# Eleven joint additions in place of fourteen, and shorter lookups, in the expert routing of a hybrid encoder layer

## The chip, the cores and the metric

The kernel runs on one core of one Trainium2 chip. The time is the device time of one execution in microseconds (us); lower is better. A core has a matrix engine (TensorE, PE in the profile; PEld is its weight load), a vector engine (VectorE, DVE), an activation engine (ScalarE, ACT), a general engine (GpSimd, POOL), a queue engine (SyncE, SP) and 16 DMA engines. Each engine works through its own list of instructions in order and waits on semaphores.

## The reference, cut to what matters

One layer over 1024 tokens of width 1024: layer norm, attention beside a long convolution, an output projection, layer norm, then a feed-forward part that picks experts, and a last layer norm. The change lies in the picking. For each token and each of 8 heads there are two lists of 128 scores; the 16 best of each list are summed in all pairs, and the 16 best pairs name the experts:

```python
sv, si = lax.top_k(s, PEER_TOPK)                                   # 16 of 128, two lists a head
cand = sv[:, :, 0, :, None] + sv[:, :, 1, None, :]
cidx = si[:, :, 0, :, None] * PEER_NKEYS + si[:, :, 1, None, :]    # PEER_NKEYS = 128
best, pos = lax.top_k(cand.reshape(C, PEER_HEADS, 256), PEER_TOPK)
eidx = jnp.take_along_axis(cidx.reshape(C, PEER_HEADS, 256), pos, axis=-1)
g = jax.nn.softmax(best, axis=-1)
u = u_tab[eidx]; vv = v_tab[eidx]                                  # 16384 experts of width 1024
a = gelu(einsum('chkd,cd->chk', u, xc))
out = einsum('chk,chkd->cd', g * a, vv)
```

All of it is fp32.

## The kernel before

The 1024 tokens are 8 tiles of 128. Three tiles (the gathered ones) fetch their 128 expert rows of each token from the tables by indirect DMA on POOL (`gather`): a row set arrives in one of six buffers `grow`, and VectorE makes a dot product of it (line 1262) or adds it to `gacc` (line 1270). The other five tiles (the dense ones) go through all 16384 experts: `u_part` multiplies a slice of 128 experts with the tokens on TensorE, after the slice has been split in two parts `uh` (ScalarE) and `ul` (VectorE, the helper at lines 290 to 292); the result, weighted by a table that `build_g` makes from the picked experts, is multiplied with the V table in the last part of the kernel (`weigh`, `v_group`).

The picking is `route(tt, rp, done)`, called once for each of the 8 tiles, always through tiles with one buffer each. Its work is on VectorE almost alone:

- lines 1022 to 1027: the 16 best values `r_sv` and their numbers `r_si` in each of 16 lists of 128 scores, by two rounds of MAX8, FIND_INDEX8 and one MATCH_REPLACE8;
- lines 1031 and 1036: the numbers cast to fp32 (`r_sf`), those of the first list times 128;
- lines 1037 to 1045: of the 256 pairs only the 50 can be among the best 16 whose ranks a, b (from 0) have (a+1)(b+1) at most 16. They are laid out as seven rectangular blocks of ranks, and one addition a block writes the sums to `r_cand`, another the expert numbers to `r_cidx`;
- lines 1048 to 1053: the 16 best of the 50 and their positions `r_pos`;
- lines 1059 to 1067: lookup of the expert number at each position: a comparison of all positions 0 to n-1 with the position wanted, a product with the numbers, and a sum (`r_oh`, `r_ef`). The best four can only lie in the first 16 candidates, the next four in the first 32;
- from line 1069: the softmax, and for a dense tile the numbers in the form that `build_g` needs.

`route` is a generator: it hands back the control after each piece, and `weights` interleaves the pieces with those of `build_g`, paced against the first 72 of the 128 calls of `u_part`. The first routing runs beside the last scores; the other seven run beside those 72 slices, first those of the dense tiles, then those of two gathered tiles. That order in the program is only a start: `TileContext(nc, schedule_with_timeline_sim=True)` lets a planner order each engine's list by its own estimate of when things are ready, and place the waits. After the 72 slices, the kernel goes on with the remaining 56, the weighting (`gt` loads the table) and the V table.

Of the kernel before, what the change touches and what calls it, by code (L numbers as in the profile page):

```python
# [10 lines left out]
F32 = mybir.dt.float32  # L11
# [5 lines left out]
ALU = mybir.AluOpType  # L17
AX = mybir.AxisListType
# [3 lines left out]
P = 128  # L22
# [273 lines left out]
def layer(ctx: ExitStack, tc: tile.TileContext, a: dict, out: bass.AP):  # L296
    nc = tc.nc
# [268 lines left out]
    for j in (*range(4, 12), *range(4)):  # L566
        u = pjp.tile([P, T], F32, name="u", bufs=1)
        project(4 + j, u)
        y = z_sb[:, j] if j < 4 else pjp.tile([P, T], F32, name="gt_y", bufs=1)
        nc.scalar.activation(y, u, AF.Identity, bias=sb[:, j:j + 1], scale=sw[:, j, 1:2])  # L570
        nc.vector.scalar_tensor_tensor(y[:, 1:T], u[:, 0:T - 1], sw[:, j, 0:1], y[:, 1:T],
                                       op0=ALU.mult, op1=ALU.add)
        nc.vector.scalar_tensor_tensor(y[:, 0:T - 1], u[:, 1:T], sw[:, j, 2:3], y[:, 0:T - 1],
                                       op0=ALU.mult, op1=ALU.add)
# [158 lines left out]
    with tc.tile_pool(name="ltp", bufs=2, side="right") as ltp:  # L733
# [70 lines left out]
        for c in range(2):  # L804
# [6 lines left out]
            for tt in range(0, NT, 2):  # L811
                ps = bank()
                for e in range(2):
                    s = slice((tt + e) * P, (tt + e + 1) * P)
# [110 lines left out]
    iota = keep.tile([P, P], F32, name="iota")  # L925
# [78 lines left out]
    NEG = -3.0e38  # L1004
    NCAND = 50

    blocks = [(0, 4, 0, 4), (0, 2, 4, 4), (4, 4, 0, 2), (0, 1, 8, 8), (8, 8, 0, 1), (2, 1, 4, 1), (4, 1, 2, 1)]
    finds = [(0, 8, 0, 4, 16), (0, 8, 4, 8, 32), (0, 4, 8, 16, NCAND), (4, 8, 8, 16, NCAND)]  # L1010

    routed = []
    CHUNK = 55.0 / 12
# [1 line left out]
    def route(tt, rp, done):  # L1015


        s = rp.tile([P, 16, P], F32, name="r_s")
        nc.sync.dma_start(s, s_d[tt].rearrange("p h (q n) -> p (h q) n", q=2))
        sv = rp.tile([P, 16, 16], F32, name="r_sv")  # L1020
        si = rp.tile([P, 16, 16], U32, name="r_si")
        for g in range(16):
            nc.vector.max(sv[:, g, 0:8], s[:, g])
            nc.vector.max_index(si[:, g, 0:8], sv[:, g, 0:8], s[:, g])
            nc.vector.match_replace(s[:, g], sv[:, g, 0:8], s[:, g], NEG)
            nc.vector.max(sv[:, g, 8:16], s[:, g])
            nc.vector.max_index(si[:, g, 8:16], sv[:, g, 8:16], s[:, g])
            if g % 3 == 2:
                yield CHUNK
        sf = rp.tile([P, 16, 16], F32, name="r_sf")  # L1030
        nc.vector.tensor_copy(sf, si)
        cand = rp.tile([P, 8, NCAND], F32, name="r_cand")
        cidx = rp.tile([P, 8, NCAND], F32, name="r_cidx")
        sv4 = sv.rearrange("p (h q) k -> p h q k", q=2)
        sf4 = sf.rearrange("p (h q) k -> p h q k", q=2)
        nc.vector.tensor_scalar(sf4[:, :, 0], sf4[:, :, 0], 128.0, None, op0=ALU.mult)
        for eng, dst, src in ((nc.vector, cand, sv4), (nc.vector, cidx, sf4)):
            off = 0
            for a0, na, b0, nb in blocks:
                o = dst[:, :, off:off + na * nb].rearrange("p h (x y) -> p h x y", y=nb)  # L1040
                x = src[:, :, 0, a0:a0 + na].unsqueeze(3).to_broadcast([P, 8, na, nb])
                y = src[:, :, 1, b0:b0 + nb].unsqueeze(2).to_broadcast([P, 8, na, nb])
                eng.tensor_add(o, x, y)
                off += na * nb
            assert off == NCAND
        best = rp.tile([P, 8, 16], F32, name="r_best")
        pos = rp.tile([P, 8, 16], U32, name="r_pos")
        for h in range(8):
            nc.vector.max(best[:, h, 0:8], cand[:, h])
            nc.vector.max_index(pos[:, h, 0:8], best[:, h, 0:8], cand[:, h])  # L1050
            nc.vector.match_replace(cand[:, h], best[:, h, 0:8], cand[:, h], NEG)
            nc.vector.max(best[:, h, 8:16], cand[:, h])
            nc.vector.max_index(pos[:, h, 8:16], best[:, h, 8:16], cand[:, h])
            if h % 4 == 3:
                yield CHUNK
        pf = rp.tile([P, 8, 16], F32, name="r_pf")
        nc.vector.tensor_copy(pf, pos)
        ef = rp.tile([P, 8, 16], F32, name="r_ef")
        for h0, h1, k0, k1, n in finds:
            nh, nk = h1 - h0, k1 - k0  # L1060
            oh = rp.tile([P, 32 * NCAND], F32, name="r_oh")[:, 0:nh * nk * n]
            oh = oh.rearrange("p (h k n) -> p h k n", h=nh, k=nk)
            nc.vector.tensor_tensor(
                oh, iota[:, 0:n].unsqueeze(1).unsqueeze(1).to_broadcast([P, nh, nk, n]),
                pf[:, h0:h1, k0:k1].unsqueeze(3).to_broadcast([P, nh, nk, n]), op=ALU.is_equal)
            nc.vector.tensor_mul(oh, oh, cidx[:, h0:h1, 0:n].unsqueeze(2).to_broadcast([P, nh, nk, n]))
            nc.vector.reduce_sum(ef[:, h0:h1, k0:k1], oh, axis=AX.X)
            yield CHUNK
        w = rp.tile([P, 8, 16], F32, name="r_w")
        nc.vector.tensor_sub(w, best, best[:, :, 0:1].to_broadcast([P, 8, 16]))  # L1070
        nc.scalar.activation(w, w, AF.Exp)
        den = rp.tile([P, 8], F32, name="r_den")
        nc.vector.reduce_sum(den, w, axis=AX.X)
        nc.vector.reciprocal(den, den)
        den_b = den.unsqueeze(2).to_broadcast([P, 8, 16])
        ef2 = ef.rearrange("p h k -> p (h k)")
        if tt < NG:
            nc.vector.tensor_copy(eid[tt], ef2)
            nc.vector.tensor_mul(gat[tt].rearrange("p (h k) -> p h k", k=16), w, den_b)
            routed.append(tt)  # L1080
            return
        nc.vector.tensor_mul(w, w, den_b)
        ei = rp.tile([P, P], I32, name="r_ei")
        nc.vector.tensor_copy(ei, ef2)
        ij = rp.tile([P, 2, P], I32, name="r_ij")
        nc.vector.tensor_scalar(ij[:, 0], ei, 7, None, op0=ALU.arith_shift_right)
        nc.vector.tensor_scalar(ij[:, 1], ei, 127, None, op0=ALU.bitwise_and)
        ijf = rp.tile([P, P], F32, name="r_ijf")
        nc.vector.tensor_copy(ijf, ij[:, 0])
        jj = rp.tile([P, P], I32, name="r_jj")  # L1090
        nc.vector.tensor_tensor(jj, ij[:, 1], ij[:, 1], op=ALU.mult)
        jp = rp.tile([P, 2, P], I32, name="r_jp")
        nc.vector.tensor_scalar(jp[:, 1], jj, 127, None, op0=ALU.bitwise_and)
        nc.vector.tensor_scalar(jp[:, 0], jj, 127 << 7, None, op0=ALU.bitwise_and)
        jx = rp.tile([P, 3, P], BF16, name="r_jx")
        nc.vector.tensor_copy(jx[:, 0], ij[:, 1])
        nc.vector.tensor_copy(jx[:, 1:3], jp)
        nc.sync.dma_start(jx_d[tt].rearrange("r t s -> t r s"), jx)
        jl = jls[tt % 2]
        for r in range(3):  # L1100
            nc.sync.dma_start(jl[32 * r:32 * r + 32], jx_d[tt, r].rearrange("(q t) s -> t q s", t=32))
        ps = psO.tile([P, 2, P], F32, name="ps_o0")
        nc.tensor.transpose(ps[:, 0], ijf, ident)
        nc.tensor.transpose(ps[:, 1], w.rearrange("p h k -> p (h k)"), ident)
        ig = rp.tile([P, 2, P], F32, name="ig", bufs=2)
        nc.scalar.copy(ig, ps)
        done.append((ig, jl))
        yield CHUNK
# [196 lines left out]
    with tc.tile_pool(name="rp", bufs=1, side="left") as rp, \  # L1305
# [9 lines left out]
        for jl in jls:  # L1315
            nc.gpsimd.memset(jl[96:98], 1.0)
        r0 = route(0, rp, [])
        for _ in scores(hd, NG, DENSE):
            with tc.issue_after(normed[-1].ins):
# [7 lines left out]
        def weights():  # L1327


            done = []  # L1330
            yield from route(NG, rp, done)
            for t in range(DENSE):
                beside = route(NG + t + 1, rp, done) if t + 1 < DENSE else route(1, rp, done)
                for n, c in enumerate(build_g(done[t], t, gp)):
                    yield c
                    if n % 5 in (0, 2, 4):
                        yield next(beside, 0.0)
                yield from beside
            for g in range(2, NG):
                yield from route(g, rp, done)  # L1340
# [214 lines left out]
```

## Time and profile before

| | us |
|---|---|
| median of 3 runs | 3274.26 |
| lowest and highest | 3264.43, 3280.19 |
| profiled execution, its own time | 3255.75 |
| span of the profile, first to last instruction | 3254.0 |

The profile is of one execution. Busy times are sums over instructions of an engine; TensorE's matmuls overlap one another, and their ends are modelled. The granted TensorE clock over the span is 0.962 of full speed. 44798 instructions were recorded, 5514 of them on VectorE.

### The profile page before, as it was taken

Reading aid. Unit: us, or ns where it says so; the run is one execution under the profiler, and the core shown is the slowest. Engines: PE = TensorE matmul, PEld = TensorE weight load, DVE = VectorE, ACT = ScalarE, POOL = GpSimd, SP = SyncE. Lnnn points to the kernel's source line nnn. Section 1 sums busy time; section 2 is a strip of 40 time slices with the busy share of each in tenths; the row PEclk is TensorE's granted clock in tenths of the full one; section 3 lists DMA queues with packets and bytes.
Section 4 is the critical chain, followed back from the end, with each engine's and each line's share of the span. In section 5 each row is a group of like instructions: output and inputs, shape, how many; then the busy total and the mean of one; then the engine's idle time right before and its main releaser. Section 6 shows DMA issues by size and latency. Waiting matters only on the chain.

```text
span 3254.0 us, 44798 instructions
## 1 busy us (share of the span) xinstructions
PE 2988.5 (92%) x15582; PEld 2552.1 (78%) x15582; DVE 2735.7 (84%) x5514; ACT 1256.2 (39%) x2454; POOL 1036.4 (32%) x797
## 2 busy tenths in 40 slices
PE   6999898889999779999999789998999999799997
PEld 5677676556689778999898778886888888588886
DVE  7556799888757799999999768888889879888888
ACT  4544344455523216766574122222222222122222
POOL 0000000000000351332435735555555445455551
PEclk9999889989999989999999899999999999999998
DMA  5244743322444777887888999999999999989995
GB/s 173 97 149 133 249 123 104 102 56 73 138 152 149 278 252 241 302 303 277 310 284 319 364 338 336 325 358 341 329 358 323 353 315 333 337 302 353 342 332 188
DMA packets 355064, 828.87 MB, mean 255 GB/s; under 512 B 34345, under 2 KB 144851, under 8 KB 351253
## 3 DMA queue, kind: packets, MB, share of 16 engines
q0 software_dynamic: 110592, 402.70, 34.5%
q1 hardware_dynamic: 230709, 356.71, 33.9%
q10 hardware_dynamic: 13536, 66.59, 5.2%
q8 instruction: 123, 2.02, 0.2%
q14 instruction: 104, 0.85, 0.1%
HBM read 715.52 MB, written 110.33 MB: 254 GB/s over the span
## 4 chain that ended last, share of the span: by engine, by line
PE 31%; DVE 22%; DMA 7%; issue 6%; POOL 3%; ACT 1%; SPq 0%; DVEq 0%; POOLq 0%; ACTq 0%
PE ps_x L285 5%; PE ps_x L287 5%; PE ps_x L286 5%; DVE grow L1262 4%; DVE gacc L1270 4%; DMA vr<-in_peer_v 3%; PE ps_h L285 3%; PE ps_h L287 3%; PE ps_h L286 3%; POOL grow L1249 3%; DVE p L1160 2%; PE ps_o L285 2%; PE ps_o L286 2%; PE ps_o L287 2%; DVE ul L292 2%
## 5 line engine op out<-in xcount | busy, mean ns | idle before, releaser
L1249 POOL DMA_INDIRECT grow<-in_peer_u,eid x384 | 518.0, 1349 | 582.3 <-DVE grow L1262 206.9
L1249 POOL DMA_INDIRECT grow<-in_peer_v,eid x384 | 504.8, 1315 | 606.1 <-DVE gacc L1270 267.3
L1270 DVE SCALAR_TENSOR_TENSOR gacc<-grow,dot,gacc 128x1024 f32<-128x1024 f32 x381 | 487.3, 1279 | 13.2 <-DMA grow<-in_peer_v,eid 9.6
L1262 DVE SCALAR_TENSOR_TENSOR grow<-grow,gh 128x1024 f32<-128x1024 f32 x384 | 460.1, 1218 | 19.8 <-DMA grow<-in_peer_u,eid 19.5
L287 PE MATMUL ps_x<-hd,ul 128*128 128x320 f32 x1152 | 368.3, 328 | 50.1 <-DVE ul L292 49.7
L285 PE MATMUL ps_x<-hd,uh 128*128 128x320 f32 x1152 | 373.6, 325 | 28.4 <-ACT uh L291 26.2
L286 PE MATMUL ps_x<-hd,uh 128*128 128x320 f32 x1152 | 370.3, 322 | 0.0
L286 PE MATMUL ps_x<-vl,wh 128*128 128x512 f32 x864 | 341.1, 395 | 1.7 <-DVE vl L292 1.6
L287 PE MATMUL ps_x<-vh,wl 128*128 128x512 f32 x864 | 336.8, 393 | 0.0
L285 PE MATMUL ps_x<-vh,wh 128*128 128x512 f32 x864 | 302.3, 396 | 28.4 <-ACT vh L291 23.2
L291 ACT CAST vh<-vr 128x512 fp32r<-128x512 f32 x256 | 156.3, 619 | 388.4 <-DMA vr<-in_peer_v 280.6
L285 PE MATMUL ps_h<-hd,uh 128*128 128x320 f32 x896 | 278.8, 311 | 9.0 <-ACT A L1221 5.6
L286 PE MATMUL ps_h<-hd,uh 128*128 128x320 f32 x896 | 278.3, 311 | 0.0
L287 PE MATMUL ps_h<-hd,ul 128*128 128x320 f32 x896 | 275.8, 311 | 2.5 <-DVE ul L292 2.5
L287 PEld LDWEIGHTS ps_x<-hd,ul 128*128 128x128 f32 x1152 | 222.7, 195 | 65.0 <-DVE ul L292 59.0
L285 PEld LDWEIGHTS ps_x<-hd,uh 128*128 128x128 f32 x1152 | 225.9, 196 | 35.4 <-ACT uh L291 31.8
L292 DVE TENSOR_TENSOR vl<-vr,vh 128x512 fp32r<-128x512 f32 x256 | 174.5, 687 | 75.7 <-ACT vh L291 74.4
L286 PEld LDWEIGHTS ps_x<-hd,uh 128*128 128x128 f32 x1152 | 225.8, 196 | 0.8
L291 ACT CAST uh<-ur 128x1024 fp32r<-128x1024 f32 x128 | 134.7, 1052 | 223.7 <-DMA ur<-in_peer_uT 103.1
L285 PEld LDWEIGHTS ps_x<-vh,wh 128*128 128x128 f32 x864 | 162.7, 190 | 63.5 <-ACT vh L291 24.7
L292 DVE TENSOR_TENSOR ul<-ur,uh 128x1024 fp32r<-128x1024 f32 x128 | 155.5, 1215 | 63.8 <-ACT uh L291 62.4
L286 PEld LDWEIGHTS ps_x<-vl,wh 128*128 128x128 f32 x864 | 164.4, 190 | 37.1 <-DVE vl L292 4.4
(366 smaller groups left out, 6876.3 us busy)
## 6 DMA issues: line engine op xcount, KB each, us to landing
ur<-in_peer_uT SPq DMA_DIRECT2D x128, 512.0 KB
vr<-in_peer_v SPq DMA_DIRECT2D x256, 256.0 KB
g_d<-gst ACTq DMA_DIRECT2D x20, 2048.0 KB
gt<-g_d SPq DMA_DIRECT2D x32, 1280.0 KB
a_d<-A ACTq DMA_DIRECT2D x72, 320.0 KB
A<-a_d SPq DMA_DIRECT2D x72, 320.0 KB
fw<-in_dft_fw SPq DMA_DIRECT2D x64, 256.0 KB
wr<-in_w_in SPq DMA_DIRECT2D x16, 512.0 KB
```

The costliest lines, as they stand in the source:

```text
L285: nc.tensor.matmul(out, L[0], R[0], start=start, stop=False)
L286: nc.tensor.matmul(out, L[0], R[1], start=False, stop=False)
L287: return nc.tensor.matmul(out, L[1], R[0], start=False, stop=stop)
L291: nc.scalar.copy(hi, src)
L292: return nc.vector.tensor_sub(lo, src, hi)
L1160: nc.vector.tensor_tensor(p1, iota.unsqueeze(1).to_broadcast([P, NB, P]), ig[:, 0, c:c + NB].unsqueeze(2).to_broadcast([P, NB, P]), op=ALU ...
L1249: nc_i = nc.gpsimd.indirect_dma_start(out=t, out_offset=None, in_=a["peer_" + kind], in_offset=bass.IndirectOffsetOnAxis(ap=eid[g][:, k:k ...
L1262: nc.vector.scalar_tensor_tensor(t, t, 1.0, h_t, op0=ALU.mult, op1=ALU.mult, accum_out=d[:, k - k0:k - k0 + 1])
L1270: nc.vector.scalar_tensor_tensor(acc, t, dots[k0][:, k - k0:k - k0 + 1], acc, op0=ALU.mult, op1=ALU.add)
```

## The change

The values and the numbers of a list now lie in one tile (`vn`, for each head the values of both lists and then the numbers of both), and so do the candidates and their expert numbers (`cc`). An addition over 16 groups (8 heads, values and numbers) writes both at once. The 50 pairs are cut into eleven blocks instead of seven and ordered so that the ranks up to 4, 8, 12 and 16 lie in the first 16, 24, 40 and 50 candidates; the lookups go by four ranks for all 8 heads. Before, the last eight ranks were looked up over all 50 candidates in two halves of the heads.

```diff
-    blocks = [(0, 4, 0, 4), (0, 2, 4, 4), (4, 4, 0, 2), (0, 1, 8, 8), (8, 8, 0, 1), (2, 1, 4, 1), (4, 1, 2, 1)]
-    finds = [(0, 8, 0, 4, 16), (0, 8, 4, 8, 32), (0, 4, 8, 16, NCAND), (4, 8, 8, 16, NCAND)]
+    blocks = [(0, 4, 0, 4), (0, 1, 4, 4), (4, 4, 0, 1), (1, 1, 4, 4), (4, 4, 1, 1), (0, 1, 8, 4), (8, 4, 0, 1),
+              (0, 1, 12, 4), (12, 4, 0, 1), (2, 1, 4, 1), (4, 1, 2, 1)]
+    finds = [(0, 4, 16), (4, 8, 24), (8, 12, 40), (12, 16, NCAND)]
...
-        sv = rp.tile([P, 16, 16], F32, name="r_sv")
+        vn = rp.tile([P, 8, 2, 2, 16], F32, name="r_sv")
         for g in range(16):
-            nc.vector.max(sv[:, g, 0:8], s[:, g])
+            sv = vn[:, g // 2, 0, g % 2]
+            nc.vector.max(sv[:, 0:8], s[:, g])
...
-        sf = rp.tile([P, 16, 16], F32, name="r_sf")
-        nc.vector.tensor_copy(sf, si)
-        cand = rp.tile([P, 8, NCAND], F32, name="r_cand")
-        cidx = rp.tile([P, 8, NCAND], F32, name="r_cidx")
-        nc.vector.tensor_scalar(sf4[:, :, 0], sf4[:, :, 0], 128.0, None, op0=ALU.mult)
-        for eng, dst, src in ((nc.vector, cand, sv4), (nc.vector, cidx, sf4)):
-            for a0, na, b0, nb in blocks:
-                eng.tensor_add(o, x, y)
+        nc.vector.tensor_copy(vn[:, :, 1], si.rearrange("p (h q) k -> p h q k", q=2))
+        nc.vector.tensor_scalar(vn[:, :, 1, 0], vn[:, :, 1, 0], 128.0, None, op0=ALU.mult)
+        cc = rp.tile([P, 8, 2, NCAND], F32, name="r_cand")
+        vn3, cc3 = vn.rearrange("p h v q k -> p (h v) q k"), cc.rearrange("p h v n -> p (h v) n")
+        for a0, na, b0, nb in blocks:
+            nc.vector.tensor_add(
+                cc3[:, :, off:off + na * nb].rearrange("p g (x y) -> p g x y", y=nb),
+                vn3[:, :, 0, a0:a0 + na].unsqueeze(3).to_broadcast([P, 16, na, nb]),
+                vn3[:, :, 1, b0:b0 + nb].unsqueeze(2).to_broadcast([P, 16, na, nb]))
+        cand, cidx = cc[:, :, 0], cc[:, :, 1]
...
-        for h0, h1, k0, k1, n in finds:
-            oh = oh.rearrange("p (h k n) -> p h k n", h=nh, k=nk)
+        for k0, k1, n in finds:
+            oh = oh.rearrange("p (h k n) -> p h k n", h=8, k=nk)
```

The three operations of a lookup stay, over all 8 heads and four ranks.

## Rows read from the trace of the kernel before

**Rows 1.** The page, busy us, share and count of each engine.

```profile
PE 2988.5 (92%) x15582; PEld 2552.1 (78%) x15582; DVE 2735.7 (84%) x5514; ACT 1256.2 (39%) x2454; POOL 1036.4 (32%) x797
```

**Rows 2.** Table by stretches: length; PE, PEld, DVE, ACT, POOL busy; clock, DMA share, GB/s.

```profile
1000.00:1047.00 47.00, 45.54 (x286) 43.66 (x285) 44.92 (x228) 17.63 (x32) 0.00 (x0) 1.00 0.40 131
...
1098.00:1735.00 637.00, 576.13 (x3944) 552.21 (x3943) 634.18 (x1971) 356.45 (x957) 226.71 (x173) 0.96 0.81 286
1735.00:1912.00 177.00, 145.44 (x903) 137.71 (x903) 139.78 (x159) 49.22 (x92) 108.84 (x78) 0.94 0.92 339
1912.00:3200.00 1288.00, 1237.62 (x6256) 1076.58 (x6255) 1109.41 (x1495) 335.52 (x557) 678.20 (x508) 0.98 0.96 336
```

**Rows 3.** Waits of DVE, 1100 to 1735 us, longest: total us, times, longest.

```profile
DVE dot L1266 <- ACT dot L1265: 1.0, 1, 1.0
...
```

**Rows 4.** Waits of PE, 1100 to 1735 us, longest in total.

```profile
PE ps_x L287 <- DVE ul L292: 36.2, 14, 6.9
...
```

**Rows 5.** Timeline of DVE, single places: start us, duration us, instruction, count.

```profile
1024.38 0.21 DVE L1036 TENSOR_SCALAR r_sf<-r_sf 128x128 f32<-128x128 f32 x1
1024.51 0.20 DVE L1049 MAX8 r_best<-r_cand 128x8 f32<-128x50 f32 x1
...
1025.68 0.98 DVE L1043 TENSOR_TENSOR r_cidx<-r_sf 128x128 f32<-128x128 f32 x7
1026.58 0.08 DVE L1051 MATCH_VALUE_LOAD r_cand<-r_best,r_cand 128x8 f32 x1
...
1039.83 1.82 DVE L1063 TENSOR_TENSOR r_oh<-iota,r_pf 128x1600 f32<-128x1600 f32 x1
1041.69 1.82 DVE L1066 TENSOR_TENSOR r_oh<-r_oh,r_cidx 128x1600 f32<-128x1600 f32 x1
...
1738.02 0.68 DVE L1063 TENSOR_TENSOR r_oh<-iota,r_pf 128x512 f32<-128x512 f32 x1
1738.62 0.20 DVE L1074 RECIPROCAL r_den<-r_den 128x8 f32<-128x8 f32 x1
...
1755.40 1.82 DVE L1063 TENSOR_TENSOR r_oh<-iota,r_pf 128x1600 f32<-128x1600 f32 x1
1757.14 1.28 DVE L1270 SCALAR_TENSOR_TENSOR gacc<-grow,dot,gacc 128x1024 f32<-128x1024 f32 x1
```

**Rows 6.** Groups by shape, DVE, 1050 to 1790 us: busy us, mean ns, idle before.

```profile
L1067 DVE TENSOR_REDUCE r_ef<-r_oh 128x32 f32<-128x1600 f32 x15 | 27.1, 1806 | 0.0
...
L1063 DVE TENSOR_TENSOR r_oh<-iota,r_pf 128x1600 f32<-128x1600 f32 x14 | 25.4, 1816 | 0.0
...
L1043 DVE TENSOR_TENSOR r_cand<-r_sv 128x64 f32<-128x64 f32 x28 | 5.4, 204 | 0.0
...
L1043 DVE TENSOR_TENSOR r_cand<-r_sv 128x8 f32<-128x8 f32 x14 | 1.8, 159 | 0.0
```

**Rows 7.** Line 1043, DVE, 1050 to 1790 us: duration ns, first and last start us.

```profile
L1043 DVE TENSOR_TENSOR r_cand<-r_sv x49: 150/203/278, 1104.2 to 1675.7; 128x64 f32<-128x64 f32 x28, 128x8 f32<-128x8 f32 x14, 128x128 f32<-128x128 f32 x7
...
```

**Rows 8.** Timeline of DVE and SP around the last routing.

```profile
1682.00 0.86 DVE L1049 MAX8 r_best<-r_cand 128x8 f32<-128x50 f32 x7
...
1713.64 1.81 DVE L1066 TENSOR_TENSOR r_oh<-r_oh,r_cidx 128x1600 f32<-128x1600 f32 x1
...
1726.67 0.38 DVE L1043 TENSOR_TENSOR r_cidx<-r_sf 128x64 f32<-128x64 f32 x3
...
1777.38 1.23 DVE L1262 SCALAR_TENSOR_TENSOR grow<-grow,gh 128x1024 f32<-128x1024 f32 x1 [4.18 <-DMA grow<-in_peer_u,eid]
...
1783.78 0.22 DVE L1078 CAST eid<-r_ef 128x128 int32<-128x128 f32 x1
...
1912.15 9.23 SPq L1368 DMA_DIRECT2D gt<-g_d  x2
```

**Rows 9.** Waits of PE, 1912 to 3200 us, the two largest.

```profile
PE ps_x L285 <- ACT vh L291: 23.2, 4, 10.0
PE ps_o L285 <- ACT vh L291: 14.5, 4, 5.7
...
```

More of the change, by code (lines that the diff above doesn't have):

```diff
@@ L1019, in route @@
         nc.sync.dma_start(s, s_d[tt].rearrange("p h (q n) -> p (h q) n", q=2))
-        sv = rp.tile([P, 16, 16], F32, name="r_sv")
+        vn = rp.tile([P, 8, 2, 2, 16], F32, name="r_sv")
         si = rp.tile([P, 16, 16], U32, name="r_si")
         for g in range(16):
-            nc.vector.max(sv[:, g, 0:8], s[:, g])
[L1024 to L1027, printed above, removed]
+            sv = vn[:, g // 2, 0, g % 2]
+            nc.vector.max(sv[:, 0:8], s[:, g])
+            nc.vector.max_index(si[:, g, 0:8], sv[:, 0:8], s[:, g])
+            nc.vector.match_replace(s[:, g], sv[:, 0:8], s[:, g], NEG)
+            nc.vector.max(sv[:, 8:16], s[:, g])
+            nc.vector.max_index(si[:, g, 8:16], sv[:, 8:16], s[:, g])
@@ L1028, in route @@
             if g % 3 == 2:
                 yield CHUNK
-        sf = rp.tile([P, 16, 16], F32, name="r_sf")
-        nc.vector.tensor_copy(sf, si)
-        cand = rp.tile([P, 8, NCAND], F32, name="r_cand")
-        cidx = rp.tile([P, 8, NCAND], F32, name="r_cidx")
-        sv4 = sv.rearrange("p (h q) k -> p h q k", q=2)
-        sf4 = sf.rearrange("p (h q) k -> p h q k", q=2)
-        nc.vector.tensor_scalar(sf4[:, :, 0], sf4[:, :, 0], 128.0, None, op0=ALU.mult)
-        for eng, dst, src in ((nc.vector, cand, sv4), (nc.vector, cidx, sf4)):
-            off = 0
-            for a0, na, b0, nb in blocks:
-                o = dst[:, :, off:off + na * nb].rearrange("p h (x y) -> p h x y", y=nb)
-                x = src[:, :, 0, a0:a0 + na].unsqueeze(3).to_broadcast([P, 8, na, nb])
-                y = src[:, :, 1, b0:b0 + nb].unsqueeze(2).to_broadcast([P, 8, na, nb])
-                eng.tensor_add(o, x, y)
-                off += na * nb
-            assert off == NCAND
+        nc.vector.tensor_copy(vn[:, :, 1], si.rearrange("p (h q) k -> p h q k", q=2))
@@ new lines, in route @@
+        nc.vector.tensor_scalar(vn[:, :, 1, 0], vn[:, :, 1, 0], 128.0, None, op0=ALU.mult)
+        cc = rp.tile([P, 8, 2, NCAND], F32, name="r_cand")
+        vn3, cc3 = vn.rearrange("p h v q k -> p (h v) q k"), cc.rearrange("p h v n -> p (h v) n")
+        off = 0
+        for a0, na, b0, nb in blocks:
[3 more added lines that the diff above has]
+                vn3[:, :, 1, b0:b0 + nb].unsqueeze(2).to_broadcast([P, 16, na, nb]))
+            off += na * nb
@@ L1046, in route @@
+        assert off == NCAND
+        cand, cidx = cc[:, :, 0], cc[:, :, 1]
         best = rp.tile([P, 8, 16], F32, name="r_best")
@@ L1058, in route @@
         ef = rp.tile([P, 8, 16], F32, name="r_ef")
-        for h0, h1, k0, k1, n in finds:
-            nh, nk = h1 - h0, k1 - k0
-            oh = rp.tile([P, 32 * NCAND], F32, name="r_oh")[:, 0:nh * nk * n]
-            oh = oh.rearrange("p (h k n) -> p h k n", h=nh, k=nk)
+        for k0, k1, n in finds:
+            nk = k1 - k0
+            oh = rp.tile([P, 32 * NCAND], F32, name="r_oh")[:, 0:8 * nk * n]
+            oh = oh.rearrange("p (h k n) -> p h k n", h=8, k=nk)
             nc.vector.tensor_tensor(
[L1064 to L1067, printed above, removed]
+                oh, iota[:, 0:n].unsqueeze(1).unsqueeze(1).to_broadcast([P, 8, nk, n]),
+                pf[:, :, k0:k1].unsqueeze(3).to_broadcast([P, 8, nk, n]), op=ALU.is_equal)
+            nc.vector.tensor_mul(oh, oh, cidx[:, :, 0:n].unsqueeze(2).to_broadcast([P, 8, nk, n]))
+            nc.vector.reduce_sum(ef[:, :, k0:k1], oh, axis=AX.X)
             yield CHUNK
```

## The prediction

> **What bounds the kernel now.** The page first: over the whole span TensorE is busy 92% and VectorE 84%, which leaves open which of them sets the time where the routing runs [rows 1]. The table by stretches answers that [rows 2]. From 1098 to 1735 us VectorE is busy 634.18 of 637 us: 2.8 us idle. TensorE is busy 576.13 us and the 16 DMA engines 0.81 of the time. The waits say the same: in that stretch VectorE's longest wait for anybody is 1.0 us [rows 3], while TensorE waits 36.2 us, in 14 pieces, for VectorE's `ul` split [rows 4]. A stretch in which one in-order engine never pauses lasts as long as its instructions take; what is taken out of its queue comes out of the stretch, until another engine is full. TensorE has 61 us to give first.
>
> Before it (1000 to 1047 us, where the first of the eight routings runs) TensorE is busy 45.54 of 47 us. After it come two stretches with other limits: 1735 to 1912 us, where the DMA engines are at 0.92 and TensorE is idle 32 us, and 1912 to 3200 us, where TensorE is busy 1237.62 of 1288 us and VectorE 1109.41 [rows 2].
>
> **The change part by part.** The price of an instruction in a full queue is the distance from its start to the next start, not its duration, since neighbours overlap. From two lookups [rows 5]: 512 elements take 1738.62-1738.02 = 0.60 us, 1600 take 1757.14-1755.40 = 1.74. That is (1.74-0.60)/1088 = 1.048 ns an element. By that line 1024 elements cost 1.14, 768 cost 0.60+256x1.048 = 0.87 and 1280 cost 0.60+768x1.048 = 1.40.
>
> *Lookups.* A routing has four blocks of comparison, product and sum. Before: 512, 1024, 1600, 1600 elements, 0.60+1.14+1.74+1.74 = 5.22 us for one of the three operations. After: 512, 768, 1280, 1600, that is 0.60+0.87+1.40+1.74 = 4.61. The comparison and the sum have the same duration within 1% [rows 6], and the product lasts as long as the comparison ahead of it, 1.82 us [rows 5], so a routing saves 3x0.61 = 1.83 us. The count of instructions stays at twelve.
>
> *Additions.* Seven of them, over 400 elements, ran back to back from 1025.68 to 1026.58, 0.90 us [rows 5]: 400x1.048 = 0.42 for the elements, 0.48/7 = 0.069 us fixed for each. Fourteen cost 1.80 us. Eleven over 800 elements (one of 256, eight of 64, two of 16) cost 0.84+11x0.069 = 1.60. Saved: 0.20 us a routing. No row has an addition into the combined tile. From one side: if instructions did not overlap, the durations would count, 0.20 and 0.16 us for 64 and 8 elements [rows 6] and by the slope 0.27 for 128, 2x(0.27+4x0.20+2x0.16) = 2.78 before against about 0.40+8x0.20+2x0.17 = 2.34 after, a saving of 0.44. From the other: if each addition had to wait for the one before, it would pay what a dependent pair pays, 1041.69-1039.83 = 1.86 against 1.74 [rows 5], 0.12 more, 11x0.12 = 1.3 us, a loss of 1.1 us a routing. I take 0.20: the seven in 0.90 us write interleaved columns of one tile, as the eleven will, and none waited.
>
> The Trainium skill ("VectorE: DVE Perf Modes", section "The TRN2 errata — SBUF-src ops pay a fixed extra latency per instruction") warns that many small instructions each pay a fixed cost, tabled as 58 cycles (60 ns), while its formula for a single fp32 addition has 151 cycles (157 ns). The seven additions agree with the smaller figure (69 ns), and what the page warns of falls here from fourteen payments to eleven. By the larger figure alone the additions would save 3x0.157 = 0.47 us a routing, and the whole change about 2 us more, an estimate from that page.
>
> *Cast and the factor 128.* They now write and read runs with gaps. The multiplication already works on runs of 16 with gaps, and its 128 elements cost 1024.51-1024.38 = 0.13 us [rows 5]: less the fixed 0.07 that is 0.06, twice the rate of the additions. So gaps did not slow it, and I take no change; if they cost the cast of 256 elements that rate, it would be 256x0.5 ns = 0.13 more a routing, 0.9 us in all. The selections keep count and sizes; only their addresses change. No DMA is added, removed or moved, and neither SP's nor POOL's queue is passed by anything.
>
> *What of it lies on the path.* The first routing saves its 2.0 us beside a TensorE that is busy 45.54 of 47 us [rows 2]: nothing. Without that cover it would be 2.0 more. The other seven add from 1104.2 us on [rows 7]; six of them make additions and lookups between 1098 and 1735 us, the seventh its additions (the last at 1726.67) and its lookups from 1738.02 on [rows 5, 8], where VectorE then waits 4.18 us for a gathered row at 1777.38 [rows 8]. So its 1.83 us are taken as nothing; without that wait they count. Sum: 6x1.83+7x0.20 = 12.4 us. TensorE's 61 idle us fall to about 49, so it does not become the bound; the DMA share goes from 0.81 to 0.81x637/625 = 0.83.
>
> *What is late next.* Gathered rows are freed by VectorE, so each gather in that stretch starts up to 12 us sooner; the stretch at 0.92 DMA then begins sooner with the same work left, and TensorE's long stretch behind it too. I take the 12.4 us as kept to the end. Bounds: all additions dependent, 6x1.83-7x1.1-0.9 = 2.4 us; no overlap and the seventh routing counted, 7x1.83+7x0.44 = 15.9 us.
>
> *An added wait.* Candidates and their numbers now share a tile of one buffer, so a routing's additions must come behind the last lookup product of the routing before. Today the candidates' last addition of the seventh routing stands at 1675.7 [rows 7], its selection starts at 1682.00, and that product runs from 1713.64 to 1715.38 [rows 8]: the selection would start some 35 us later. Both are on VectorE, in one in-order queue, so nothing stands still while other work is ready; what is queued behind (gathers, splits) moves ahead instead. Who needs the result? The last routing ends at 1783.78, the long stretch's first load of the weights `gt` is issued at 1912.15 [rows 8]: 128 us of room.
>
> The profiled execution took 3255.75 us (span 3254.0), 18.5 us under the median of the runs, 3274.26. Taken from the profile: 3255.75-12.4 = 3243.4, 0.38% less. By the same share the median goes to 3262.
>
> **The rivals.** *Absorbed.* The 12 us reappear as waiting for copies between 1735 and 1912 us. For it: DMA share 0.92 there, and TensorE waits there anyway. Against: the gathers before it shift by the same amount. Time: 3274.
>
> *Order redrawn for the worse.* The order of every engine's list is made by a planner from its own estimates, so other lengths can move instructions that the diff doesn't name. The place where it costs is 1912 to 3200 us, where TensorE's idle time is few and large waits: eight for `vh`, 37.7 us [rows 9]. As many again would cost 38 us against a gain of 12: 3274+25 = 3299. It decides from about 12 us of new waits, four of today's mean of 4.7 being 19. For it: TensorE is the bound there, nothing gives the loss back. Against: the V loads and their splits are not touched.
>
> *Order redrawn for the better.* The same, but the 32 idle us of TensorE in 1735 to 1912, which come with gathers crowded at 78 in 177 us against 173 in 637 before [rows 2], go by half: 12+16 = 28 us less, 3246; all of it, 44 less, 3230.
>
> *The hand-over binds.* If each of six hand-overs cost the 35 us of the last one, 210 us stand against 128 of room: 82-12 = 70 slower, 3344. It decides from 128+12 = 140 us of delay, 23 a hand-over. Against: VectorE is never idle in that stretch, so a late selection is work done later, not time lost, until the room is used up.
>
> **How the numbers follow.** Gain kept: 0.47, time 3262, own range by the bounds 3258 to 3272. Absorbed: 0.18. Redrawn worse: 0.15. Redrawn better: 0.15. Hand-over: 0.05. The kernel's runs differ by 0.5% (3264.43 to 3280.19), about what can be told from no change; that is 16 us. Faster by more than that means below 3258: nearly all of the redrawn better (0.13), and a part of the gain kept where the run adds to it (0.13): 0.26. Slower means above 3290: three quarters of redrawn worse (0.11) and the hand-over: 0.16. Within: 0.58. The range goes from 3236, most of the better case, to 3299, half of the worse; what is left out is the hand-over, half of the worse case and a third of the better one, under 0.2.
>
> **What would show it.** Twelve lookup instructions a routing with about 0.94 us for 768 and 1.48 for 1280 elements (those durations less the overlap are 0.87 and 1.40); eleven additions of 0.16 to 0.41 us each; VectorE still without idle time in the saturated stretch, which ends near 1723 instead of 1735; TensorE's wait for `ul` smaller by some 10 us; the first V matmuls some 12 us sooner. Wrong, if the stretch shortens and the long stretch's start does not move (absorbed), if additions start 1.86-like distances apart (dependent), or if TensorE's waits after 1912 us change by more than the 12 us (order redrawn).

## The result and the profile after

| | before | after |
|---|---|---|
| median of 17 runs each, us | 3265.91 | 3285.62 |
| lowest and highest | 3256.91, 3280.19 | 3273.99, 3309.76 |
| profiled execution, span | 3255.75, 3254.0 | 3280.22, 3278.0 |

The ratio after to before is 1.006, 95% interval 1.0047 to 1.0073: slower by 0.6%, 20 us. The prediction was 3262, 0.38% faster, from a median of before of 3274.26 (three runs; seventeen gave 3265.91), with chances of 0.26 for faster than the scatter of the runs, 0.58 for a difference within it and 0.16 for slower.

First the work itself. The page of after, busy us of each engine, answers to [rows 1]:

```profile
PE 2998.1 (91%) x15582; PEld 2551.6 (78%) x15582; DVE 2721.1 (83%) x5490; ACT 1253.4 (38%) x2454; POOL 1072.1 (33%) x797
```

VectorE has 24 instructions fewer, three for each of the eight routings, and 14.6 us less to do. The first routing of after, places from VectorE's timeline (start us, duration us, instruction, count), answers to [rows 5]:

```profile
1024.46 1.71 DVE L1039 TENSOR_TENSOR r_cand<-r_sv 128x256 f32<-128x256 f32 x11
1026.20 0.66 DVE L1049 MAX8 r_best<-r_cand 128x8 f32<-128x50 f32 x5
...
1036.30 0.95 DVE L1063 TENSOR_TENSOR r_oh<-iota,r_pf 128x768 f32<-128x768 f32 x1
...
1040.28 1.49 DVE L1063 TENSOR_TENSOR r_oh<-iota,r_pf 128x1280 f32<-128x1280 f32 x1
```

Eleven additions in 1.71 us, the new lookup sizes in 0.95 and 1.49: as priced. So the work was saved, and the kernel is slower. The stretches of after (length; PE, PEld, DVE, ACT, POOL busy; clock, DMA share, GB/s) answer to [rows 2]:

```profile
1098.00:1735.00 637.00, 574.45 (x3899) 543.12 (x3898) 624.45 (x1901) 350.60 (x949) 271.95 (x181) 0.97 0.82 290
1735.00:1912.00 177.00, 145.42 (x915) 138.50 (x913) 136.43 (x214) 51.68 (x100) 97.40 (x72) 0.94 0.88 322
1912.00:3200.00 1288.00, 1228.80 (x6190) 1067.99 (x6191) 1094.80 (x1474) 329.71 (x548) 677.94 (x507) 0.98 0.95 334
```

The stretch that should have become shorter did not give TensorE a faster feed: in the same 637 us it is busy 574.45 us (576.13 before). VectorE is busy 624.45 instead of 634.18: part of what it saved is now idle time (12.55 us where it had 2.8). Its waits there (1100 to 1735 us: total us, times, longest), and TensorE's, answer to [rows 3, 4]:

```profile
DVE grow L1262 <- DMA grow<-in_peer_u,eid: 9.3, 7, 2.6
```

```profile
PE ps_x L287 <- DVE ul L292: 36.5, 22, 5.9
```

VectorE now arrives at gathered rows before they have landed, while TensorE waits for VectorE's `ul` split as long as before. The last routing and the first load of `gt`, answering to [rows 8]:

```profile
1715.11 0.28 DVE L1033 CAST r_sv<-r_si 128x256 f32<-128x256 uint32 x1
...
1720.58 0.22 DVE L1034 TENSOR_SCALAR r_sv<-r_sv 128x128 f32<-128x128 f32 x1
1720.72 1.82 DVE L1066 TENSOR_TENSOR r_oh<-r_oh,r_cand 128x1600 f32<-128x1600 f32 x1
...
1727.18 1.60 DVE L1039 TENSOR_TENSOR r_cand<-r_sv 128x256 f32<-128x256 f32 x10
1728.70 1.28 DVE L1270 SCALAR_TENSOR_TENSOR gacc<-grow,dot,gacc 128x1024 f32<-128x1024 f32 x1
1729.89 0.18 DVE L1039 TENSOR_TENSOR r_cand<-r_sv 128x16 f32<-128x16 f32 x1
1729.99 1.22 DVE L292 TENSOR_TENSOR ul<-ur,uh 128x1024 fp32r<-128x1024 f32 x1
...
1733.91 0.43 DVE L1049 MAX8 r_best<-r_cand 128x8 f32<-128x50 f32 x3
...
1799.25 0.33 DVE L1078 CAST eid<-r_ef 128x128 int32<-128x128 f32 x1
...
1916.52 9.47 SPq L1368 DMA_DIRECT2D gt<-g_d  x2
```

The added wait is there: the additions of the last routing stand behind the last lookup product of the one before, and its selection starts at 1733.91 instead of 1682.00. The change also adds a second wait, which the prediction doesn't name: a joint addition needs the numbers as well as the values. In before the last addition of the values stood at 1675.7 us [rows 7], ahead of the cast of the numbers:

```profile
1681.69 0.39 DVE L1031 CAST r_sf<-r_si 128x256 f32<-128x256 uint32 x1
```

In after the additions come behind the cast (1715.11) and the factor 128 (1720.58) too. The routing ends 15 us later, the long stretch begins only 4 us later. TensorE's waits for `vh` from 1912 to 3200 us, answering to [rows 9], are 38.3 us in all (37.7 before):

```profile
PE ps_x L285 <- ACT vh L291: 25.4, 10, 9.7
PE ps_o L285 <- ACT vh L291: 12.9, 4, 6.7
```

So the loss is neither in the long stretch's large waits nor in its start. It is in how much was left to do then. From 1912 us to the end TensorE of after is still busy for

```profile
1912.00:3300.00 1388.00, 1290.21 (x6456) 1117.61 (x6456) 1151.59 (x1560) 350.85 (x582) 680.23 (x508) 0.97 0.90 317
```

1290.21 us, where before it was

```profile
1912.00:3300.00 1388.00, 1274.96 (x6420) 1107.17 (x6418) 1150.09 (x1559) 349.33 (x579) 678.20 (x508) 0.98 0.90 317
```

1274.96: 15 us of the 24 by which the two profiled spans differ. The other 9 are idle time of TensorE there (3278.0-1912-1290.2 = 75.8 us, 67.0 before). Each is one execution; a second execution of the same two lists, shown below, gives 16 and 2 us, so only the first of the two parts is firm.

### The profile page after: what moved, and what is told of

It is laid out like the page before. It is cut to its first block, busy times and chain, and to the rows that moved or that the text cites. A ratio compares the mean times of both kernels' runs of the same rounds, so it can differ in the third digit from the quotient of the medians.

```text
span 3278.0 us, 44794 instructions
## 1 busy us (share of the span) xinstructions
PE 2998.1 (91%) x15582; PEld 2551.6 (78%) x15582; DVE 2721.1 (83%) x5490; ACT 1253.4 (38%) x2454; POOL 1072.1 (33%) x797
## 5 line engine op out<-in xcount | busy, mean ns | idle before, releaser
L1249 POOL DMA_INDIRECT grow<-in_peer_v,eid x384 | 530.0, 1380 | 583.7 <-DVE gacc L1270 246.0
L1249 POOL DMA_INDIRECT grow<-in_peer_u,eid x384 | 528.2, 1375 | 574.0 <-DVE grow L1262 169.3
L1270 DVE SCALAR_TENSOR_TENSOR gacc<-grow,dot,gacc 128x1024 f32<-128x1024 f32 x381 | 487.9, 1281 | 14.9 <-DMA grow<-in_peer_v,eid 11.6
L285 PE MATMUL ps_x<-hd,uh 128*128 128x320 f32 x1152 | 372.2, 324 | 30.0 <-ACT uh L291 29.8
L1166 ACT ACTIVATE p<-ps_o,ig 128x128 f32<-128x128 f32 x640 | 189.1, 427 | 17.3 <-PE ps_o L1153 17.1
```

Source lines behind the costliest of these rows:

```text
L285: nc.tensor.matmul(out, L[0], R[0], start=start, stop=False)
L1166: nc.scalar.activation(p2[:, j], ps[:, j], AF.Relu, scale=ig[:, 1, c + j:c + j + 1])
L1249: nc_i = nc.gpsimd.indirect_dma_start(out=t, out_offset=None, in_=a["peer_" + kind], in_offset=bass.IndirectOffsetOnAxis(ap=eid[g][:, k:k ...
L1270: nc.vector.scalar_tensor_tensor(acc, t, dots[k0][:, k - k0:k - k0 + 1], acc, op0=ALU.mult, op1=ALU.add)
```

## The experiments

Two theories run through them. *Hand-over*: the shared candidate tile delays each routing, VectorE takes gathered rows meanwhile, the slices come late. *Draw*: the planner makes another order of every engine's list whenever anything changes, and orders differ by more than this change is worth.

**Parts of the change, one by one.** A second buffer for the shared tile (e1_two_bufs); the eleven blocks and the lookups by rank on the old separate tiles, 22 additions (e2_lookups_only); the joint tiles with the old seven blocks and old lookups (e3_joint_only); and after with a rule that ties a gathered row's VectorE work to the slices (e6_pin, explained below).

```diff
# e1_two_bufs, on after
-        cc = rp.tile([P, 8, 2, NCAND], F32, name="r_cand")
+        cc = rp.tile([P, 8, 2, NCAND], F32, name="r_cand", bufs=2)
# e2_lookups_only, on before: blocks and finds of after
# e3_joint_only, on after: blocks and finds of before
```

> The changed kernel with two buffers for the joint candidate tile, so that a routing's additions no longer wait for the last lookup product of the routing before. Hand-over theory: the late second selection let gathers run ahead of the slices; with it gone the second selections start within 10 us of the former places (1178.6, 1273.0, 1389.1 us ...), the 56th slice is stored before 1730 us and the time is 0.3 to 0.5% under the kernel before (ratio 0.995 to 0.997). Redrawn-order theory: any other order is a new draw, the ratio may be anything from 0.994 to 1.010 and does not follow the selection's place.

> The kernel before with the eleven blocks and the four lookups by rank alone: values and numbers in separate tiles, 22 additions a routing. By the prices of the prediction a routing saves 1.83 us in lookups and pays 0.56 us for eight more additions: about 1.3 us, 9 us over seven routings. Hand-over theory: separate tiles, no hand-over, ratio 0.996 to 0.999. Redrawn-order theory: anything from 0.994 to 1.010.

> The joint tiles and joint additions alone, with the former seven blocks and the former lookups: seven additions a routing instead of fourteen, 0.48 us saved, 3.4 us over seven. Hand-over theory: the hand-over is there in full and little is saved, so it is as slow as the changed kernel or slower, ratio 1.005 to 1.010. Redrawn-order theory: anything from 0.994 to 1.010.

> The changed kernel, in which during the first 72 slices each gathered row's VectorE work is queued behind the split of the slice ahead of it in the program, so that gathers cannot run ahead of slices. Both theories hold that what costs is gathers ahead of slices (114 loads against 102 at the 32nd slice): if so, the 56th slice is stored some 20 us sooner than 1743 us and the 71st before 1887; whether the later stage pays it back with more gathers left is open, the ratio 0.990 to 1.003. If gathers ahead of slices are not the cause, the ratio stays at 1.006.

| us | median | lowest, highest | ratio to before, rebuilt |
|---|---|---|---|
| before, built anew | 3313.53 | 3303.48, 3320.73 | 1 |
| e1_two_bufs | 3265.21 | 3255.11, 3277.44 | 0.986 [0.9835, 0.9885] |
| e2_lookups_only | 3289.73 | 3282.84, 3295.64 | 0.9932 [0.9911, 0.9952] |
| e3_joint_only | 3268.3 | 3261.65, 3275.39 | 0.9859 [0.9836, 0.9881] |
| e6_pin | 3248.94 | 3245.43, 3261.68 | 0.9816 [0.9792, 0.984] |

The line that matters is the first. The unchanged text of before, built once more, took 3313.53 us, 1.5% above its own 3265.91. A difference of 0.6% between two texts means little if one text has two times; none of these four times can be laid to its edit, and the expected ratios, which were meant against 3266, decide nothing.

**Holding the draw.** The text has one place whose outcome it doesn't fix. `run_net`, the helper that writes out the long convolution's additions, gives two temporaries back in the order of a Python set of names, and that order changes from one build to the next:

```diff
-        for q in {a, b}:
+        for q in sorted({a, b}, key=lambda q: crc32(repr((q, DRAW)).encode())):
```

Which of two buffers is used again sets which addition waits for which, and from there the planner orders everything anew. No instruction comes or goes. Pair order 1 (DRAW 2) gives TensorE's list of the profiled before and of the profiled after, place for place; order 2 (DRAW 0) gives a list that leaves order 1's after the first 580 of 15582 matmuls, 172 us into the kernel, and differs from it at 7562 places. The traces of the four kernels above show that the order did change between builds: up to the first routing e1_two_bufs has the matmul list of order 3 (below), the other three that of order 2. There is no trace of the rebuilt before.

> The kernel before, with one line of the network helper made definite: the loop that frees two temporaries runs over an unordered pair, so a build may hand out the buffers in either order, and the planner then makes another list for every engine. Here the pair's order is fixed to the one under which the lists are those of the profiled before. No instruction is added or removed. Both theories: 3266 within 10, the time of the many runs of before.

> The kernel after, the pair's order fixed in the same way; its lists are those of the profiled after. Both theories: 3286 within 10, slower than before_o1 by 0.6%.

> The kernel before, the pair fixed the other way round at some places: the same instructions in other lists. Theory 'hand-over' (the shared candidate tile delays each routing, gathered rows run ahead of the slices, and that costs 0.6%): the pair's order has nothing to do with the routing, so this stays within 0.3% of before_o1, 3256 to 3276. Theory 'draw' (any change that makes the planner redraw the lists moves the time by about 1% either way, whatever it saves): 0.5 to 1.5% away from before_o1, either sign, that is below 3250 or above 3282.

> The kernel after, the pair fixed as in before_o2. 'Hand-over': 0.6% slower than before_o2, within 0.3%. 'Draw': its distance from before_o2 is unlike 0.6%, by 0.5% or more, and may have the other sign.

| us | order 1 | order 2 |
|---|---|---|
| before | 3265.96 (3259.67 to 3266.96) | 3292.63 (3279.23 to 3307.32) |
| after | 3285.23 (3283.0 to 3291.09) | 3265.99 (3262.0 to 3273.64) |
| after / before | +0.6% | -0.8% |

All four on one chip, beside the rebuilt before at 3312.86. The sign of the change turns with the order in which temporaries of the convolution are given back, and its last addition starts at 802 us, before the routing begins. So the 0.6% belongs to the draw. 'Hand-over' failed twice: it wanted before_o2 at 3256 to 3276 us and after_o2 0.6% slower than that. Within one order, before and after share the first 3968 matmuls on TensorE, up to 1035 us in the first routing, and differ at about half of the places behind it (6152 of 11614 under order 1).

Two things can be read from the pairs all the same, each from one execution a kernel. The first is where the saved time goes. VectorE's instructions on gathered rows (tile `grow`), 1098 to 1440 us, kernels before_o1 and after_o1 (length; DVE busy and count; clock, DMA share, GB/s):

```profile
1098.00:1440.00 342.00, 112.53 (x138) 0.93 0.79 275
```

```profile
1098.00:1440.00 342.00, 129.49 (x167) 0.95 0.81 287
```

and those on the slices' split (tile `ul`), in the same order:

```profile
1098.00:1440.00 342.00, 36.32 (x30) 0.93 0.79 275
```

```profile
1098.00:1440.00 342.00, 36.31 (x30) 0.95 0.81 287
```

Thirty slices in both; the freed time, and what the delayed selections leave, goes to 17.0 us more of gathered rows. Order 2 shows the same (29 splits in both; rows 111.45 and 124.34 us), and so does order 3 below (30 and 29; 113.53 and 126.34). By 1735 us, behind six of the seven routings, 10.3, 8.5 and 10.4 us of the surplus are left (210.73 and 221.07 us under order 1), at 53 splits in every after and 52 or 53 in before: about what six routings save. TensorE's waits in this stretch name the slices' splits above all, and never a gathered row. But this holds for all three pairs, and two of them are faster after the change: it says why the stretch gained nothing, not why the measured pair got slower.

The second is what a draw is made of. From 1912 us to the end TensorE's list has so much left, and stands idle so long (length of the window, which reaches past the end; PE, PEld, DVE, ACT, POOL busy; clock, DMA share, GB/s). Of before_o1, after_o1, before_o2 and after_o2, one fence each:

```profile
1912.00:3300.00 1388.00, 1280.58 (x6459) 1110.92 (x6457) 1151.48 (x1560) 351.67 (x582) 678.89 (x508) 0.98 0.90 318
```

```profile
1912.00:3300.00 1388.00, 1296.69 (x6515) 1123.35 (x6513) 1152.65 (x1561) 353.43 (x585) 681.92 (x508) 0.98 0.90 318
```

```profile
1912.00:3300.00 1388.00, 1282.70 (x6417) 1112.10 (x6416) 1147.95 (x1559) 349.35 (x578) 682.87 (x508) 0.97 0.90 316
```

```profile
1912.00:3300.00 1388.00, 1285.78 (x6508) 1117.48 (x6507) 1153.60 (x1561) 352.42 (x585) 682.70 (x508) 0.98 0.90 318
```

The spans are 3264.2, 3282.7, 3277.5 and 3260.2 us. Less 1912 and the busy time, TensorE idles 71.6, 74.0, 82.8 and 62.4 us. Under order 1 the change adds 16.1 us of work left and 2.4 of idle time; under order 2 it adds 3.1 of work and takes 20.4 of idle time away. Before_o3 and after_o3 of the third order below have

```profile
1912.00:3300.00 1388.00, 1302.86 (x6576) 1130.00 (x6574) 1162.87 (x1572) 357.03 (x590) 676.49 (x512) 0.98 0.92 321
```

```profile
1912.00:3300.00 1388.00, 1278.96 (x6468) 1110.38 (x6466) 1151.49 (x1560) 350.96 (x582) 678.98 (x508) 0.98 0.90 317
```

with spans of 3285.8 and 3251.3 us: 23.9 of work and 10.6 of idle time less. The idle time of order 2 has a place. It is TensorE's wait for `vh`, 47.1 us in before_o2 and 29.8 in after_o2 (from 1912 us to the end: total us, times, longest):

```profile
PE ps_x L285 <- ACT vh L291: 28.0, 8, 7.7
PE ps_o L285 <- ACT vh L291: 19.1, 6, 8.4
```

```profile
PE ps_x L285 <- ACT vh L291: 21.5, 5, 11.0
PE ps_o L285 <- ACT vh L291: 8.3, 5, 3.5
```

The diff names neither the V slices nor their splits.

**A rule that ties gathered rows to slices.** If the freed time is lost because it goes to rows that nobody waits for, it should come out once it can't. Until the last routing is done, VectorE's work on a row is issued only behind the `ul` split of the slice which the program had reached; it adds an order on VectorE and leaves the count of its instructions (5514 before, 5490 after):

```diff
-        split(nc, uh, ul, ur)
+        splits.append(split(nc, uh, ul, ur).ins)
...
-                use(n - LAG)
+                with tc.issue_after(splits[-1]) if early[0] else ExitStack():
+                    use(n - LAG)
```

> The kernel before, pair order 1, and one rule more: until the last routing is done, what VectorE does for a gathered row is issued only behind the `ul` split of the slice that the program had reached, so that gathered rows can't run ahead of the slices. Theory 'slices late' (what moves the time is how many of the slices' matmuls are left for the last stage when gathered rows run ahead): TensorE's busy time left behind 1912 us falls from 1281 to under 1265, and the time to 3240-3258. Theory 'draw' (the place of every instruction is redrawn, waits fall as they fall): the rule is one more redraw, the time lies anywhere from 3255 to 3300.

> The kernel after, pair order 1, with the same rule. 'Slices late': TensorE's busy time left behind 1912 us under 1265 instead of 1297, time 3235-3255, and not slower than pinned_before_o1, since less work is left for VectorE and the gathers are held back in both. 'Draw': anywhere from 3255 to 3300, and its distance to pinned_before_o1 may have either sign.

> As pinned_before_o1, with pair order 2. 'Slices late': 3240-3258, though before_o2 took 3293. 'Draw': as far from pinned_before_o1 as before_o2 from before_o1, 0.5% or more.

> As pinned_after_o1, with pair order 2. 'Slices late': 3235-3255. 'Draw': anywhere from 3255 to 3300.

**A third order** (md5 in place of crc32, DRAW 1), with and without the rule:

> The kernel before, pair order 3 (a third set of lists). 'Draw': anywhere from 3255 to 3315. 'Slices late' alone: within 10 of before_o1, since the pair's order does not touch gathers or slices.

> The kernel after, pair order 3. If the change has an effect of its own without the rule, its sign is that of the profiled pair: slower than before_o3 by 0.3 to 0.9%. 'Draw': any difference up to 1.5%, either way.

> The kernel before with the rule that holds the gathered rows to the slices, pair order 3: 3255 to 3290, as in the two others.

> The kernel after with the rule, pair order 3. If the work saved comes out under the rule (VectorE's freed time goes to the slices, not to gathered rows): 3240 to 3255, faster than pinned_before_o3 by 0.3 to 1.2%, TensorE's busy time left behind 1912 us 1245-1255. 'Draw' alone: either sign against pinned_before_o3.

All medians, us. Before and after of a row were run beside each other; the rebuilt before, which ran with each group, took 3312.86 to 3313.53:

| order | before | after | | before, rule | after, rule | |
|---|---|---|---|---|---|---|
| 1 | 3265.96 | 3285.23 | +0.6% | 3262.04 | 3251.34 | -0.3% |
| 2 | 3292.63 | 3265.99 | -0.8% | 3282.21 | 3245.47 | -1.1% |
| 3 | 3276.40 | 3253.04 | -0.7% | 3264.68 | 3237.90 | -0.8% |
| mean | 3278.3 | 3268.1 | | 3269.6 | 3244.9 | |

Against the rebuilt before the ratios under the rule are 0.9846 [0.9825, 0.9867] and 0.9813 [0.9793, 0.9832] for order 1, 0.9908 [0.9889, 0.9928] and 0.9805 [0.9781, 0.9829] for order 2, 0.9865 [0.9843, 0.9888] and 0.9786 [0.9763, 0.9809] for order 3. With the rule the change is faster in all three. e6_pin, with 3248.94, is no fourth order: its matmul list is that of pinned_after_o2, place for place. After with the rule came out below the 3255 to 3300 that 'draw' gave it under orders 1 and 2 (3251 and 3245). What the rule was made for shows in TensorE's wait for `ul`, 1100 to 1735 us, of pinned_before_o1, pinned_after_o1, pinned_before_o2 and pinned_after_o2:

```profile
PE ps_x L287 <- DVE ul L292: 36.7, 16, 7.1
```

```profile
PE ps_x L287 <- DVE ul L292: 20.1, 16, 2.6
```

```profile
PE ps_x L287 <- DVE ul L292: 33.7, 14, 4.4
```

```profile
PE ps_x L287 <- DVE ul L292: 24.0, 11, 5.3
```

Under order 3 it falls from 40.4 to 22.3 us. Without the rule it rose under orders 1 and 2 (31.9 to 32.8, 28.3 to 33.9) and fell under order 3 (45.7 to 33.8). VectorE's time on gathered rows still grows with the rule, by 10.0, 5.5 and 6.3 us by 1735 us, but now with 3, 0 and 2 more splits. The lines from 1912 us to the end of pinned_before_o1, pinned_after_o1, pinned_before_o3 and pinned_after_o3:

```profile
1912.00:3300.00 1388.00, 1267.05 (x6336) 1097.34 (x6336) 1180.44 (x1598) 350.52 (x579) 717.77 (x531) 0.97 0.92 322
```

```profile
1912.00:3300.00 1388.00, 1246.51 (x6241) 1077.53 (x6239) 1160.05 (x1567) 340.75 (x564) 700.36 (x523) 0.97 0.90 315
```

```profile
1912.00:3300.00 1388.00, 1266.08 (x6332) 1096.90 (x6330) 1172.59 (x1588) 344.72 (x571) 701.23 (x530) 0.97 0.91 320
```

```profile
1912.00:3300.00 1388.00, 1247.87 (x6260) 1081.35 (x6258) 1162.90 (x1571) 342.07 (x567) 687.11 (x524) 0.97 0.90 317
```

The change takes 20.5 and 18.2 us of TensorE's work out of the last stage (24.5 under order 2), each time. The idle time there moves by +8.7, +0.3 and, under order 2, -28.6 us, where the waits for `vh` fall from 66.1 to 26.5. So the 37 us of order 2 are in large part such waits, and the 14.6 us taken out of VectorE's list do not by themselves explain gains of 37 or 27 us. The last store of a slice's result (line of the store; duration; first and last start us) says it from the other end, for before_o1, after_o1, pinned_before_o1 and pinned_after_o1:

```profile
L1352 ACTq DMA_DIRECT2D a_d<-A x69: 326/326/344, 1102.9 to 1896.3; - x69
```

```profile
L1352 ACTq DMA_DIRECT2D a_d<-A x69: 326/326/391, 1105.9 to 1915.3; - x69
```

```profile
L1355 ACTq DMA_DIRECT2D a_d<-A x69: 326/326/363, 1103.3 to 1864.5; - x69
```

```profile
L1355 ACTq DMA_DIRECT2D a_d<-A x69: 325/326/366, 1103.6 to 1835.8; - x69
```

Without the rule the change made the 72 slices end 19 us later under order 1, 12.5 later under order 2 (where the kernel was 27 us faster) and 13 sooner under order 3; with it they end 29, 20 and 13 us sooner. When the slices end does not alone set the time. For before with the rule the expectation of 'slices late' failed: 1267 and 1273 us of work left under orders 1 and 2 instead of under 1265, and 3262 and 3282 us instead of 3240 to 3258. The rule alone ends the slices of before 32, 37 and 66 us sooner and gives only 4, 10 and 12 us: the rows held back are made later (VectorE's work behind 1912 us goes from 1151.5 to 1180.4 us under order 1). The change gives 11, 37 and 27 on top.

**The hand-over.** What is left of the first theory: a second buffer under orders 1 and 2.

> The kernel after with two buffers for the shared candidate tile, pair order 1; nothing else. 'Hand-over': the wait is gone, so 3253 within 8, the time that the saved work gives under before_o1. 'Draw': anywhere from 3250 to 3295, no tie to after_o1's 3285.

> The same with pair order 2. 'Hand-over': faster than after_o2 (3266) as well, and within 8 of two_bufs_o1. 'Draw': anywhere from 3250 to 3295.

| us | after | with a second buffer |
|---|---|---|
| order 1 | 3285.23 | 3295.57 (3279.97 to 3305.91), ratio to the rebuilt before 0.9957 [0.9941, 0.9972] |
| order 2 | 3265.99 | 3256.02 (3251.77 to 3260.94), ratio 0.9843 [0.9821, 0.9864] |

The wait for the buffer is gone. The first round of selections (duration; first and last start us), after_o1 and two_bufs_o1:

```profile
L1049 DVE MAX8 r_best<-r_cand x56: 185/195/209, 1124.0 to 1738.2; 128x8 f32<-128x50 f32 x56
```

```profile
L1049 DVE MAX8 r_best<-r_cand x56: 181/189/246, 1118.9 to 1710.5; 128x8 f32<-128x50 f32 x56
```

Its last one starts at 1710.5 instead of 1738.2 us; in before_o1 it was 1693.7, and the wait for the numbers stays. The time rises by 10 us in one order and falls by 10 in the other; e1_two_bufs, which began with order 3's list, took 3265 where after_o3 took 3253. 'Hand-over' wanted 3245 to 3261 under order 1, and the two within 8 of each other; they are 40 apart. That theory falls; what the hand-over costs, if anything, can't be told here from a draw. The best kernel of all is after with the rule under order 3, 3237.9 us, 0.9% under the 3266 of before.

## Why the prediction was wrong, point by point

*Price of the lookups and additions: right.* 768 and 1280 elements were forecast at 0.94 and 1.48 us and took 0.95 and 1.49. The additions were forecast at 1.60 us for eleven; 1.71 were measured, with the last one's full duration in it, and the first selection that needs them starts 1.74 us after the first addition: by that 0.06 us are saved a routing where 0.20 were forecast. In the last routing ten take 1.52 us (1727.18 to 1728.70) and the eleventh, later, 0.10: 1.62. The bound in which every addition waits for the one before (1.3 us more) is excluded. On the warning that the prediction takes from the Trainium skill ("VectorE: DVE Perf Modes", section "The TRN2 errata — SBUF-src ops pay a fixed extra latency per instruction") the trace stays with the smaller figure: 0.84 us for the elements plus eleven times 60 ns would be 1.50, eleven times 157 ns would be 2.57, both estimates with that page's figures. In all VectorE has 14.6 us less to do; the prediction's savings, 1.83+0.20 over eight routings, make 16.2.

*"What is taken out of its queue comes out of the stretch": this is the step that failed.* The stretch is limited by VectorE, as [rows 3, 4] show, but a stretch isn't one row of work. VectorE's list there mixes splits for which TensorE waits with gathered rows that could come any time up to the end of the kernel. What is saved goes to whichever the list has next, and that was rows: 9 to 10 us more of them by 1735 us in three pairs, with the same splits or one more, and in the measured pair 9.3 us of idle time when the rows ran ahead of their transfers. TensorE's wait for `ul`, which should have fallen by some 10 us, stayed (36.2 and 36.5). The prediction had the thought, in its added wait, that gathers and splits move ahead instead, and did not ask which of the two. With the rule, under which no row can pass the split ahead of it, that wait falls by 10 to 18 us in all three pairs, TensorE has 18 to 25 us less left for the last stage, and the change gives 11, 37 and 27 us; forecast were 12.4. That the rows take the time was seen in all three pairs; that this is why the saving does not come out rests on the rule, which is itself a redraw, and three pairs with the same sign.

*"I take the 12.4 us as kept to the end": wrong for the measured pair.* TensorE's work left behind 1912 us rose by 15 to 16 us under its order. That it came out slower is the order it was built in: with two other orders the same edit is 0.7 and 0.8% faster. Over three orders the change without the rule gives 10 us on the mean, near to the forecast, but with single results of +19, -27 and -23 that mean shows nothing by itself.

*The order redrawn: the right rival, with too little chance.* Its two sides had 0.30 together. Three orders and a rebuild of the unchanged text put before at 3266, 3276, 3293 and 3313 us, a spread of 1.4%, and after at 3253 to 3285. Any forecast within 0.5% for an edit that the planner sees was too narrow; the range, 3236 to 3299, held the time because of this rival alone. Its place was given as the waits for `vh`. In the measured pair they stayed (38.3 and 37.7 us), and what moved is how far the slices had come; under order 2 they did move, by 17 us, and with the rule by 40.

*The hand-over: a delay came, and did not bind.* 35 us were forecast for the last routing and 52 came; it ended 15 us later, and the long stretch began 4 us later. A part of the delay is the wait for the numbers, which the prediction left out. With a second buffer the times move both ways.

*Absorbed.* Not in the place named: from 1735 to 1912 us TensorE is busy 145.4 us in both, and the DMA share fell from 0.92 to 0.88.

*What stays open.* Why one order leaves 1281 and another 1303 us of TensorE's work for the last stage (order 3, before), and which of the planner's choices move the waits for `vh`, was not traced; the orders differ at thousands of places. Whether the change without the rule is faster on the average of many orders would need more than three, and so would the size of its gain with the rule. The order in which the rebuilt before ran at 3313 us is not known.

## What to carry to other kernels

Before a difference under 1% is laid to an edit, build the unchanged text again and time that; and make every place definite that a planner can take either way, down to the order of a set. A saving in a full queue is worth what the queue does next: look for the instruction behind the one removed and ask who waits for it. If two kinds of work share the queue and only one feeds the limiting engine, tie the other to it first; here an edit that lost in one of three orders and gained in two gained in all three with the tie.

## What the runs showed of the hardware that was not expected

Little: sizes and fixed costs came as read from the trace of before. The surprise is one of scale. Another order of giving back temporaries in the long convolution, with no instruction added, moved the end of the kernel by 27 us (3265.96 and 3292.63), though the helper's last addition starts at 802 us, while the granted clock over the span stayed between 0.958 and 0.966 in the profiled executions of all fourteen kernels with a fixed order.
